# The causal corner of attention: 256 TensorE products replaced by a mask that GpSimd adds into the loaded row of F

## The chip, the cores and the metric

One core of one Trainium2 chip runs the whole program in one launch. The metric is device time in microseconds (us), from the first to the last instruction of the program on that core and what little lies around it. Five engines with a queue each matter here: TensorE (PE in the profile, PEld for its weight loads), VectorE (DVE), ScalarE (ACT), GpSimd (POOL) and the DMA queues, above all that of SyncE (SP). Each engine takes its instructions in the order of its queue. An instruction that needs another engine's result waits on a semaphore, and everything behind it in the same queue waits with it.

## The reference

The program is one layer with two branches, a Mamba-2 branch and an attention branch with 16 heads of 64, over 1024 positions and 1024 channels. Only the attention branch is touched. Cut to what matters:

```
fcum = jnp.cumsum(log_f, axis=-1)
for blk in range(seqlen // ATT_BLOCK):                 # 8 blocks of 128 queries
    q0, q1 = blk * ATT_BLOCK, (blk + 1) * ATT_BLOCK
    s = jnp.einsum('bhqd,bhkd->bhqk', q[:, :, q0:q1], k[:, :, :q1]).astype(jnp.float32) * scale
    s = s + fcum[:, :, q0:q1, None] - fcum[:, :, None, :q1]
    qpos = q0 + jnp.arange(ATT_BLOCK)
    kpos = jnp.arange(q1)
    s = jnp.where(kpos[None, :] <= qpos[:, None], s, -jnp.inf)
    prob = jax.nn.softmax(s, axis=-1)
    outs.append(jnp.einsum('bhqk,bhkd->bhqd', prob.astype(v.dtype), v[:, :, :q1]))
```

A block of 128 queries sees all earlier key blocks whole. Only in its own block, the last 128x128 corner of its scores, must the keys that lie after a query be hidden. That corner is the subject of the change.

## The kernel before

The kernel computes negated scores (q is stored times -0.125), so a hidden key must get a very large positive number, a row's best key is its minimum, and the exponential is taken of minus the score plus that minimum.

Before attention the program computes the projections and the Mamba-2 branch, until about 695 us of the profiled span. Attention then takes the heads two by two: `hp` runs from 0 to 7, and e = 0, 1 is the head of the pair, which sits on partitions 0 to 63 or 64 to 127. Inside a pair there are six groups, given by `GROUPS`: a pair of query blocks (`u` = 0 is the higher block, `u` = 1 the lower) against one half h of the keys, 512 positions. Four of the six groups are diagonal ones, where both query blocks meet their own key block: g0 (blocks 7 and 6, upper keys, 512 and 384 keys wide), g2 (blocks 5 and 4, upper keys, 256 and 128), g4 (blocks 3 and 2, lower keys, 512 and 384) and g5 (blocks 1 and 0, lower keys, 256 and 128). Groups g1 and g3 lie fully below the diagonal. So there are 32 diagonal groups in the program, and 48 in all.

One group goes through these steps. `scores` multiplies on TensorE (in three products, since q and k are each split into two parts) into PSUM tiles `s`, one for each e, first for u = 0 and then for u = 1. VectorE then runs one combined instruction for each (u, e), line 1459: it adds `fb`, the row of F for these keys, which was loaded from memory and repeated over all 128 partitions, writes `ex`, and leaves the row's minimum in `nm`. ScalarE takes the exponential in place and sums it (line 1463). `turned` transposes `ex` on TensorE into tiles `pt`, which VectorE (line 1481) or ScalarE (line 1483) copy to `p`, and `weighted` multiplies them with v into `av`. The transposes of the first key block need the four `ex` of the group in the order u0 e0, u0 e1, u1 e0, u1 e1.

So that TensorE is not idle while VectorE and ScalarE work on a group, the program puts pieces of an independent stream of matrix products between the steps: `fill(m, 0)` between the scores and the transposes, `fill(m, 1)` between the transposes and `weighted`. Such a piece is called a half: six products 512 wide. The stream needs its own copies on the other engines, which share their queues with attention: ScalarE empties PSUM (`s<-pb`, line 404) and rounds weights (`wop<-raw`, `wop<-sum`, line 351), VectorE forms the remainders (line 352) and sums (lines 357, 373, 381) and combines results (lines 414 to 418); in the later head pairs it also splits operands (`x..h`, `x..l`, lines 277 to 281).

A softmax needs the sums over both key halves. `send` transposes the factors (`tp`), ScalarE copies them (`st`), GpSimd sends them to memory (`st_dram`, line 1387), SP loads them back repeated (`rb`, line 1393), and VectorE multiplies the output with them (lines 1418 and 1424, then 1425 for `zr`). Two groups after the scores this must be done. GpSimd also writes `zr` to memory (`ya_dram`, line 1514), forms differences of blocks (lines 213, 1520, 1526, 1527, 1540) and stores them (line 195, 1060).

The causal corner is made on TensorE: after the three products of a diagonal tile come two more products for each e, 64 rows by 128 columns in bf16, of a piece of the unit matrix `eye` with a piece of `far`, which holds 1e30 above the diagonal. They add the corner to the scores in PSUM (lines 1447 to 1453). `eye` and `far` are made once, at lines 1293 to 1306.

A scheduler in the language sets the order of each engine's queue from the program's order and its own estimate of times. Instructions that go through `pin` or `mm` keep the program's order among themselves; the others, those of the stream among them, are placed by the scheduler, so that a change of the program can move them.

## Time and profile before

| what | value |
|---|---|
| median of 3 runs | 1339.51 us (1337.2 to 1344.38) |
| profiled execution, span from first to last instruction | 1338.1 us |
| TensorE busy | 1273.1 us, 95% of the span |
| VectorE busy | 1016.8 us, 76% |
| ScalarE busy | 787.4 us, 59% |
| GpSimd busy | 303.6 us, 23% |
| the 256 corner products (`s<-far,eye`) | 18.6 us busy, mean 225 ns |
| mean granted TensorE clock | 0.988 |

The page gives no time of the profiled execution other than its span, 1.4 us under the median. Busy times of TensorE are sums over pipelined instructions: the next product starts before the one ahead has ended, so what a product costs is read from start to start and not from its length. A row of the timeline has the start, the length, engine, line, operation and tiles, how many like instructions were merged into it, and in brackets the idle time of the engine ahead of it with what ended it. A row of the table by stretches has for each engine the busy time and the count of its instructions.

### The profile page before, as it was taken

Reading aid. Unit: us, or ns where it says so; the run is one execution under the profiler, and the core shown is the slowest. Engines: PE = TensorE matmul, PEld = TensorE weight load, DVE = VectorE, ACT = ScalarE, POOL = GpSimd, SP = SyncE. Lnnn points to the kernel's source line nnn. Section 1 sums busy time; section 2 is a strip of 40 time slices with the busy share of each in tenths; the row PEclk is TensorE's granted clock in tenths of the full one; section 3 lists DMA queues with packets and bytes.
Section 4 is the critical chain, followed back from the end, with each engine's and each line's share of the span. In section 5 each row is a group of like instructions: output and inputs, shape, how many; then the busy total and the mean of one; then the engine's idle time right before and its main releaser. Section 6 shows DMA issues by size and latency. Waiting matters only on the chain. (4 is left out here: it accounts for less than half of the span.)

```text
span 1338.1 us, 21044 instructions
## 1 busy us (share of the span) xinstructions
PE 1273.1 (95%) x7054; PEld 992.6 (74%) x7054; DVE 1016.8 (76%) x1977; ACT 787.4 (59%) x1726; POOL 303.6 (23%) x311
## 2 busy tenths in 40 slices
PE   6899999999999999999999999998879998889997
PEld 4678878777888888788877777776657666668886
DVE  7979986887888888888676667666876657676976
ACT  7645765466665666566556665666754545543664
POOL 3000440013300431034002132221121213235152
PEclk9999999999999999999999999999999999889999
DMA  7232543554446533654474566567855657545933
GB/s 287 70 116 66 164 136 121 155 171 157 127 126 202 166 120 121 198 170 130 135 267 151 180 201 204 183 228 241 277 194 185 189 190 244 182 149 183 368 127 102
DMA packets 154668, 233.59 MB, mean 175 GB/s; under 512 B 17216, under 2 KB 62656, under 8 KB 154560
## 3 DMA queue, kind: packets, MB, share of 16 engines
q1 hardware_dynamic: 142016, 205.53, 48.2%
q0 software_dynamic: 6400, 16.10, 3.2%
q10 hardware_dynamic: 6144, 10.62, 2.1%
q8 instruction: 55, 0.90, 0.3%
q14 instruction: 53, 0.43, 0.1%
HBM read 162.99 MB, written 72.34 MB: 176 GB/s over the span
## 5 line engine op out<-in xcount | busy, mean ns | idle before, releaser
L1463 ACT ACTIVATE ex<-ex,nm 128x512 f32<-128x512 f32 (+1 forms) x192 | 116.0, 605 | 154.2 <-DVE nm L1459 152.3
L352 DVE TENSOR_TENSOR wop<-sum,wop 128x512 fp32r<-128x512 f32 x180 | 138.3, 769 | 54.5 <-ACT wop L351 53.4
L351 ACT ACTIVATE wop<-sum 128x512 fp32r<-128x512 f32 x180 | 112.4, 625 | 78.1 <-DVE sum L357 29.6
L352 DVE TENSOR_TENSOR wop<-raw,wop 128x512 fp32r<-128x512 f32 x144 | 110.5, 768 | 43.6 <-ACT wop L351 42.6
L404 ACT ACTIVATE s<-pb 128x512 f32<-128x512 f32 x144 | 84.9, 589 | 90.2 <-PE pb L130 87.8
L130 PE MATMUL pc<-x3h,wop 128*128 128x512 f32 x384 | 133.1, 404 | 2.8 <-DVE th L414 1.7
L130 PE MATMUL pc<-x2h,wop 128*128 128x512 f32 x384 | 130.9, 399 | 2.3 <-DVE th L416 2.0
L130 PE MATMUL pb<-x4h,wop 128*128 128x512 f32 x384 | 130.3, 396 | 2.8 <-ACT x4h L277 2.1
L130 PE MATMUL pb<-x0h,wop 128*128 128x512 f32 x384 | 132.3, 401 | 0.0
L130 PE MATMUL pb<-x5h,wop 128*128 128x512 f32 x384 | 130.7, 399 | 1.0 <-ACT s L404 1.0
L130 PE MATMUL pb<-x6h,wop 128*128 128x512 f32 x384 | 129.0, 394 | 0.0
L1459 DVE CUSTOM_DVE_ANT_0 ex<-s,fb 128x512 f32<-128x512 f32 (+1 forms) x192 | 95.7, 550 | 36.8 <-PE s L130 36.8
L133 PE MATMUL pt<-ident,ex 128*128 128x128 f32 x576 | 81.3, 283 | 20.5 <-ACT ex L1463 19.8
L351 ACT ACTIVATE wop<-raw 128x512 fp32r<-128x512 f32 x144 | 89.5, 622 | 12.4 <-PE pc L130 6.1
L130 PE MATMUL pd<-x1h,wop 128*128 128x512 f32 x288 | 96.6, 394 | 0.0
L133 PEld LDWEIGHTS pt<-ident,ex 128*128 128x128 f32 x576 | 67.7, 143 | 35.9 <-ACT ex L1463 29.9
L130 PEld LDWEIGHTS pc<-x3h,wop 128*128 128x128 f32 x384 | 73.7, 192 | 22.0 <-issue 2.6
L130 PEld LDWEIGHTS pc<-x2h,wop 128*128 128x128 f32 x384 | 72.1, 188 | 20.8 <-DVE th L416 3.1
L130 PEld LDWEIGHTS pb<-x5h,wop 128*128 128x128 f32 x384 | 73.3, 191 | 18.5 <-ACT s L404 1.7
L130 PEld LDWEIGHTS pb<-x4h,wop 128*128 128x128 f32 x384 | 72.1, 188 | 19.7 <-ACT x4h L277 2.5
L130 PEld LDWEIGHTS pb<-x0h,wop 128*128 128x128 f32 x384 | 73.5, 191 | 16.3 <-issue 0.9
L130 PEld LDWEIGHTS pb<-x6h,wop 128*128 128x128 f32 x384 | 72.1, 188 | 16.1 <-issue 0.4
(310 smaller groups left out, 2965.8 us busy)
## 6 DMA issues: line engine op xcount, KB each, us to landing
raw<-in_wu SPq DMA_DIRECT2D x128, 256.0 KB, 4.1
csb<-cs_dram SPq DMA_DIRECT2D x32, 256.0 KB, 5.2
fb<-f_dram SPq DMA_DIRECT2D x16, 512.0 KB, 6.2
rb<-st_dram SPq DMA_DIRECT2D x48, 128.0 KB, 3.1
wd<-in_wo SPq DMA_DIRECT2D x40, 128.0 KB, 3.1
xt<-in_x SPq DMA_DIRECT2D x8, 512.0 KB, 5.9
gs_dram<-th ACTq DMA_DIRECT2D x16, 256.0 KB, 3.7
qh_dram<-th SPq DMA_DIRECT2D x16, 256.0 KB, 2.0
```

The source lines that it names most:

```text
L130: return tc.keep_in_program_order(nc.tensor.matmul(*args, **kw))
L133: return tc.keep_in_program_order(nc.tensor.transpose(out_, in_, idn))
L351: nc.scalar.activation(op[:, 0], src, AF.Copy)
L352: nc.vector.tensor_tensor(op[:, 1], src, op[:, 0], ALU.subtract)
L404: nc.scalar.activation(s, ps, AF.Copy)
L1459: nc.vector.tensor_tensor_reduce(o, s[e][:, 0:w], fb[hp, h][:, e, 0:w], 1.0, 3.0e38, ALU.add, ALU.min, nm)
L1463: pin(nc.scalar.activation(o, o, AF.Exp, scale=-1.0, bias=nm, accum_out=hd.at(hd.sm, i, h, e)))
```

## The change

The corner is no longer added by TensorE. A tile `ahead` (128x128, float) holds 1e30 above the diagonal and zero elsewhere. The new function `hide` lets GpSimd add it in place into one 128-key block of the row `fb`, for one e or for both. VectorE's combined instruction then adds `fb` as before, and the mask comes with it.

Since the same row of F serves two query blocks, the moment matters: the block that is the corner for u = 0 must already be masked when u = 0 is read, and the block that is the corner for u = 1 must be masked after u = 0 has read it unmasked and before u = 1 reads it. So in each diagonal group there are two half-size additions (one for each e, 128x128) between VectorE's reads for u = 0 and u = 1, 64 in all. And there are 32 full additions (both e, 128x2x128) ahead of the groups: after the scores of g0, of g3 and of g4 for later groups of the same pair, one more after g4 for the next pair's first group, and one before the loop. What is masked stays masked: a later group of the pair does not read such a block, or needs it masked.

```
-        eye = ap.tile([P, 192], BF16, name="eye")
-        far = ap.tile([P, 192], BF16, name="far")
-        nc.vector.memset(eye, 0.0)
-        big, beyond = small("big"), small("beyond")
-        nc.vector.memset(big[:, 0:192], -NEG)
-        for e in range(2):
-            nc.vector.tensor_copy(eye[rows[e], 64:P], ident[rows[e], rows[e]])
-            nc.gpsimd.affine_select(
-                beyond[:, 192 * e : 192 * e + 192], big[:, 0:192], [[1, 192]], ALU.is_gt, 0.0, base=64 * e - 64,
-                channel_multiplier=-1,
-            )
-            nc.vector.tensor_copy(far[rows[e], :], beyond[rows[e], 192 * e : 192 * e + 192])
-        corner = [(eye[:, 64:192], far[:, 64:192]), (eye[:, 0:P], far[:, 0:P])]
+        ahead = ap.tile([P, P], F32, name="ahead")
+        big = small("big")
+        nc.vector.memset(big[:, 0:P], -NEG)
+        nc.gpsimd.affine_select(ahead, big[:, 0:P], [[1, P]], ALU.is_gt, 0.0, base=0, channel_multiplier=-1)
+
+        def hide(hp, h, block, es=slice(0, 2)):
+
+            f = fb[hp, h][:, es, block * P : block * P + P]
+            pin(nc.gpsimd.tensor_tensor(f, f, ahead.unsqueeze(1).to_broadcast([P, es.stop - es.start, P]), ALU.add))
...
-            diagonal = h == i // 4
             for m, (x, y) in enumerate(ops):
                 for e in range(2):
-                    mm(
-                        s[e][:, 0:w], x[rows[e]], y[rows[e]], start=(m == 0), stop=(m == 2 and not diagonal),
-                        skip_group_check=True,
-                    )
-            if diagonal:
-                for n, (x, y) in enumerate(corner):
-                    for e in range(2):
-                        mm(
-                            s[e][:, w - P : w], x[rows[e]], y[rows[e]], start=False, stop=(n == 1),
-                            skip_group_check=True,
-                        )
+                    mm(s[e][:, 0:w], x[rows[e]], y[rows[e]], start=(m == 0), stop=(m == 2), skip_group_check=True)
...
                 pin(nc.scalar.activation(o, o, AF.Exp, scale=-1.0, bias=nm, accum_out=hd.at(hd.sm, i, h, e)))
+                if u == 0 and h == i // 4:
+                    hide(hp, h, pair[1] % 4, slice(e, e + 1))
...
             load_v(0, h)
+        hide(0, 1, 3)
         for _ in range(14):
             stream.half()
...
             stream.release()
+            if g in (0, 4):
+                hide(hp, GROUPS[g][1], 1)
+            if g == 3:
+                hide(hp, 0, 3)
+            if g == 4 and hp + 1 < NK:
+                hide(hp + 1, 1, 3)
             for hd, which in end(m):
                 hd.settle(which)
```

The scheduler's order also changes. In the rows below, `ex,sm<-ex,nm` is the exponential, and `x2` says that two like instructions follow each other. ScalarE's queue at the first diagonal group (pair 0, g0), before:

```order
L1463 ACTIVATE ex,sm<-ex,nm 128x512 x2
L1463 ACTIVATE ex,sm<-ex,nm 128x384 x2
L404 ACTIVATE s<-pb 128x512
L351 ACTIVATE wop<-raw 128x512
L1483 ACTIVATE p<-pt 128x512 x2
```

And with the change, where the exponential is at line 1445 and the copy at line 1467:

```order
L1445 ACTIVATE ex,sm<-ex,nm 128x512 x2
L1445 ACTIVATE ex,sm<-ex,nm 128x384
L404 ACTIVATE s<-pb 128x512
L351 ACTIVATE wop<-raw 128x512
L1445 ACTIVATE ex,sm<-ex,nm 128x384
L1467 ACTIVATE p<-pt 128x512 x2
```

Two instructions of the stream now stand ahead of the group's last exponential. The same pair of instructions is moved so in pair 1, g0; in pair 6, g0 four are moved (`s<-pb`, `wop<-raw`, `th<-pb`, `wop<-raw`), two ahead of the third exponential and two ahead of the fourth; in g4 of pairs 0 to 4 and 6 one.

GpSimd's queue around pair 5, g0, before (`ya_dram<-zr` is the output's way to memory, `x` and `y` are block differences):

```order
L1060 DMA ms_dram<-th 128x512
L1514 DMA ya_dram<-zr 128x512
L1526 TENSOR_TENSOR x<-zr,x 128x512
L1527 TENSOR_TENSOR y<-x,y 128x512
L195 DMA t_a<-x 128x512
L195 DMA t_a<-y 128x512
```

And with the change, where 128x128 rows of line 1301 are the half-size additions and 128x2x128 the full ones:

```order
L1301 TENSOR_TENSOR fb<-fb,ahead 128x128 x2
L1498 DMA ya_dram<-zr 128x512
L1510 TENSOR_TENSOR x<-zr,x 128x512
L1511 TENSOR_TENSOR y<-x,y 128x512
L1301 TENSOR_TENSOR fb<-fb,ahead 128x128 x2
L1301 TENSOR_TENSOR fb<-fb,ahead 128x2x128
L195 DMA t_a<-x 128x512
L195 DMA t_a<-y 128x512
```

The two half-size additions of g0 stand behind `ya_dram`, `x` and `y`, which all wait for `zr`. The same holds in g0 of pairs 6 and 7.

VectorE's queue in pair 5, g0 (`ISA ex,nm` is the combined instruction, `ISA nm` its short second part), before:

```order
L1459 ISA ex,nm<-s,fb 128x512
L1459 ISA nm 128x1
L1459 ISA ex,nm<-s,fb 128x512
L1459 ISA nm 128x1
L357 TENSOR_TENSOR sum<-sum,raw 128x512
L1459 ISA ex,nm<-s,fb 128x384
L1459 ISA nm 128x1
L1459 ISA ex,nm<-s,fb 128x384
L1459 ISA nm 128x1
L381 TENSOR_TENSOR raw<-raw 128x512
```

And with the change, where the combined instruction is at line 1441:

```order
L1441 ISA ex,nm<-s,fb 128x512
L1441 ISA nm 128x1
L357 TENSOR_TENSOR sum<-sum,raw 128x512
L1441 ISA ex,nm<-s,fb 128x512
L1441 ISA nm 128x1
L381 TENSOR_TENSOR raw<-raw 128x512
L1441 ISA ex,nm<-s,fb 128x384
L1441 ISA nm 128x1
L1441 ISA ex,nm<-s,fb 128x384
L1441 ISA nm 128x1
```

The second sum of the stream (`raw<-raw`) has moved from behind the group's combined instructions to ahead of the last two. In pair 4, g2 an operand split moves in the same way.

## The prediction

> **What bounds the kernel now.** I read the table by stretches first, one row for each pair of heads in attention (start to end in us, then busy time of PE, PEld, DVE, ACT and POOL).
>
> ```profile
> 695.50:752.60 57.10, 57.10 (x391) 43.70 (x390) 36.57 (x99) 35.82 (x90) 8.15 (x10) 1.00 0.51 162
> 868.30:927.20 58.90, 57.54 (x393) 43.68 (x391) 39.42 (x101) 37.51 (x95) 13.82 (x18) 1.00 0.66 218
> ...
> 927.20:991.80 64.60, 54.25 (x359) 38.24 (x355) 48.93 (x119) 43.82 (x108) 9.34 (x14) 0.97 0.71 244
> 991.80:1051.60 59.80, 54.46 (x363) 39.13 (x361) 39.69 (x102) 28.98 (x80) 12.68 (x19) 0.97 0.57 189
> ...
> 1111.90:1176.00 64.10, 54.51 (x344) 38.53 (x342) 44.72 (x111) 36.98 (x96) 19.50 (x23) 0.92 0.64 210
> ```
>
> TensorE is busy 57.10 of 57.10 us in pair 0 and still 57.54 of 58.90 in pair 3: there a TensorE instruction less is time saved. In pairs 4, 5 and 7 it stands idle for 10.4, 5.3 and 9.6 us, and something else sets the pace. The table of waits for 927 to 1176 us says what (waiter, awaited: us, times, longest):
>
> ```profile
> PE pt L133 <- ACT ex L1463: 19.8, 28, 2.8
> ```
> ```profile
> DVE o L1424 <- DMA rb<-st_dram: 12.1, 5, 3.1
> ```
>
> TensorE waits for the exponentials, and these are late because VectorE first waited for the softmax factors on their way through memory. There a shorter TensorE step mostly makes a longer wait.
>
> **What goes: the corner products.** The timeline of TensorE in pair 0, at g0, g1 (no corner) and g2:
>
> ```profile
> 695.52 0.97 PE L130 MATMUL s<-k,q 64*128 64x512 f32 x6
> 696.33 0.29 PE L130 MATMUL s<-far,eye 64*128 64x128 bf16 x4
> 696.42 0.77 PE L130 MATMUL s<-k,q 64*128 64x384 f32 x6
> 697.03 0.29 PE L130 MATMUL s<-far,eye 64*128 64x128 bf16 x4
> 697.25 0.50 PE L130 MATMUL pb<-x4h,wop 128*128 128x512 f32 x1
> ...
> 706.15 1.67 PE L130 MATMUL s<-k,q 64*128 64x512 f32 x12
> 707.75 0.50 PE L130 MATMUL pb<-x5h,wop 128*128 128x512 f32 x1
> ...
> 717.06 0.62 PE L130 MATMUL s<-k,q 64*128 64x256 f32 x6
> 717.52 0.29 PE L130 MATMUL s<-far,eye 64*128 64x128 bf16 x4
> 717.62 0.53 PE L130 MATMUL s<-k,q 64*128 64x128 f32 x6
> 717.99 0.29 PE L130 MATMUL s<-far,eye 64*128 64x128 bf16 x4
> 718.21 0.50 PE L130 MATMUL pb<-x0h,wop 128*128 128x512 f32 x1
> ```
>
> From the first score product to the first of the stream, g0 takes 1.73 us, g1 1.60 and g2 1.15. Six products 512 wide take 0.81 (695.52 to 696.33), 384 wide 0.61, 256 wide 0.46, 128 wide 0.37. Without a corner g0 should take g1's time less the difference of one set, 1.60 - 0.20 = 1.40, and g2 1.60 - 0.35 - 0.44 = 0.81. So a corner costs 0.33 or 0.34 us; since part of each set's time is the change-over to the corner, I take 0.30. Four groups in eight pairs: 32 x 0.30 = 9.6 us, between 0 (all turned into waits) and 10.9 (32 x 0.34). The setup lost (two casts, two memsets for one) lies 15 us ahead of the first group, beside other work: nothing.
>
> **What comes: 64 half-size and 32 full additions on GpSimd.** No such shape is in the trace; the nearest are a GpSimd addition or product of 256 elements and one of 512.
>
> ```profile
> 571.84 0.41 DVE L839 TENSOR_TENSOR xdt<-tr,dtn 128x256 f32<-128x256 f32 x1
> ```
> ```profile
> 572.33 0.61 POOL L871 TENSOR_TENSOR xe<-xdt,tend 128x256 f32<-128x256 f32 x1 [13.82 <-DVE xdt L839]
> ...
> 581.62 1.06 POOL L892 TENSOR_TENSOR new<-new,cdec 128x256 f32<-128x256 f32 x1
> ...
> 929.12 1.29 POOL L213 TENSOR_TENSOR x<-x,th 128x512 f32<-128x512 f32 x1
> ```
> ```profile
> L1300 POOL TENSOR_SCALAR_AFFINE_SELECT beyond<-big 128x192 f32<-128x192 f32 x2 | 0.6, 346 | 48.0 <-DVE th L636 48.0
> ```
> ```profile
> 678.63 0.66 DVE L1304 CAST far<-beyond 64x192 bf16<-64x192 f32 x2 [0.45 <-POOL beyond L1300]
> ```
>
> 256 elements take 0.61 us (1.06 at worst here) and 512 take 1.29, so a full addition (256) costs 0.61 and a half-size one, by the same slope, 0.29, since nothing on VectorE that reads two SBUF tiles need stand beside it; at most 0.61. GpSimd started `xe` 0.08 us after VectorE ended `xdt` (572.25). VectorE started `far` 0.03 us after the first `beyond` ended (678.25 + 0.35). A half-size addition is thus back 0.08 + 0.29 + 0.03 = 0.40 us after VectorE has read the row. The time it has for that stands in VectorE's ladder at g0 and g2:
>
> ```profile
> 697.62 0.68 DVE L1459 CUSTOM_DVE_ANT_0 ex<-s,fb 128x512 f32<-128x512 f32 x1
> ...
> 698.23 0.69 DVE L1459 CUSTOM_DVE_ANT_0 ex<-s,fb 128x512 f32<-128x512 f32 x1
> ...
> 698.84 0.55 DVE L1459 CUSTOM_DVE_ANT_0 ex<-s,fb 128x384 f32<-128x384 f32 x1
> ```
> ```profile
> 717.89 0.41 DVE L1459 CUSTOM_DVE_ANT_0 ex<-s,fb 128x256 f32<-128x256 f32 x1
> ...
> 718.23 0.42 DVE L1459 CUSTOM_DVE_ANT_0 ex<-s,fb 128x256 f32<-128x256 f32 x1
> ...
> 718.58 0.29 DVE L1459 CUSTOM_DVE_ANT_0 ex<-s,fb 128x128 f32<-128x128 f32 x1
> ...
> 718.79 0.28 DVE L1459 CUSTOM_DVE_ANT_0 ex<-s,fb 128x128 f32<-128x128 f32 x1
> ```
>
> The e = 0 read of g0 ends at 698.30, its masked row is back at 698.70, and u = 1 starts at 698.84 anyway: no wait. At g2 it ends at 718.30, is back at 718.70, and 718.58 was the start: 0.12 us late; e = 1 is back at 718.65 + 0.40 = 719.05 for 718.79: 0.26 late. So g2 and g5 lose 0.26 us on VectorE. In pairs 0 to 3 TensorE has other work then; in pairs 4, 5 and 7 it waits for these exponentials: 6 x 0.26 = 1.6 us.
>
> **What is moved.** ScalarE's end of the first group, and TensorE's transposes after it:
>
> ```profile
> 700.38 0.60 ACT L1463 ACTIVATE ex<-ex,nm 128x384 f32<-128x384 f32 x1
> ...
> 700.98 0.58 ACT L404 ACTIVATE s<-pb 128x512 f32<-128x512 f32 x1
> 701.45 0.62 ACT L351 ACTIVATE wop<-raw 128x512 fp32r<-128x512 f32 x1
> ```
> ```profile
> 701.47 1.69 PE L133 MATMUL pt<-ident,ex 128*128 128x128 f32 x14
> ```
>
> The fourth transpose needs the last exponential; at 1.69/14 = 0.12 us each that is about 701.8, and it was ready at 700.98, 0.8 us ahead. The change lets VectorE do a sum (0.61 by the ladder's step) ahead of u = 1, and ScalarE `s<-pb` (0.47) and `wop<-raw` (0.6) ahead of the last exponential. VectorE's delay uses some 0.4 that ScalarE had left over, so the exponential is ready about 1.4 to 1.5 us later, near 702.4. TensorE then waits instead of saving: 0.6 us lost and 0.3 not gained. Pair 1, g0 has the same move, and I count the same 0.6. In pair 6, g0 `th<-pb` also stands ahead; it needs a bank that TensorE finishes just ahead of the transposes, and I count 1.4. Together 2.6 lost, 0.9 not gained: 3.5 us. The six moves in g4 (one instruction, 0.5 to 0.6 us) I cost at nothing: one such move stays within the 0.8 us of room found in g0; without that cover they cost 6 x 0.55 = 3.3. The moved sum in pair 5, g0 and the moved split in pair 4, g2 lie where TensorE waits: 2 x 0.6 = 1.2 us.
>
> GpSimd's queue is the other place. In g0 of pairs 5 to 7 the half-size additions stand behind `ya_dram`, `x` and `y`:
>
> ```profile
> 1116.97 1.27 POOL L1527 TENSOR_TENSOR y<-x,y 128x512 f32<-128x512 f32 x1
> ```
> ```profile
> 1116.66 0.56 DVE L1459 CUSTOM_DVE_ANT_0 ex<-s,fb 128x384 f32<-128x384 f32 x1
> ```
>
> In pair 7 `y` ends at 1118.24, the mask is there at 1118.56, and u = 1 would have started at 1116.66: 1.9 us of VectorE standing still, with all its queue. ScalarE already had two stream instructions (1.1 us) ahead of its last exponential there, so I put 0.8 on the path. Pair 6 is in the 1.4 above. What stands behind the additions on GpSimd is mostly the sending of the softmax factors, and this waits for ScalarE with GpSimd idle:
>
> ```profile
> POOL st_dram L1387 <- ACT st L1385: 146.9, 20, 22.9
> ```
>
> So the additions, which are due before these factors exist, cost it nothing. SP's loads move by one to three places, ten or so of them, all for a later group: nothing; no DMA is added.
>
> The full additions start right behind u = 1, when VectorE goes on with stream work:
>
> ```profile
> 928.75 2.22 DVE L352 TENSOR_TENSOR wop<-raw,wop 128x512 fp32r<-128x512 f32 x1
> ```
>
> This instruction, 0.68 elsewhere, stretched by 1.5 us while GpSimd ran the `x` of 929.12 (1.29 us): VectorE lost all of GpSimd's time. If every full addition did that, 32 x 0.61 = 19.5 us of VectorE's time; where TensorE waits (12 of them, pairs 4, 5, 7) 7.3. Not each meets such an instruction; of 7.3 I put a fifth, 1.4, on the path. [...]
>
> **The sum.** -9.6 for the corners; of these 3.6 back in pairs 4, 5 and 7 (12 x 0.30); +3.5 for ScalarE's moves in g0; +1.6 for the late masks of g2 and g5; +1.2 for VectorE's moves; +0.8 for pair 7; +1.4 for the full additions. That is +2.5 on the profiled span of 1338.1, so 1340.6; the median of the runs stands 1.4 above that span, so 1342.
>
> **The rivals.** Faster: the saving passes nearly everywhere, since the exponentials of g0 keep their room and the late pairs follow TensorE after all; 9.6 less 1.6 is 8, giving 1331. For it speak pairs 0 to 3, where TensorE never stands still; against it the g0 orders above. Slower: the mask comes back late. If a half-size addition takes the 0.61 us of the 256-element row, e = 0 is back 0.72 us after its read and e = 1 0.61 later; u = 1 is late by 0.3 in g0 and g4 and by 0.8 to 0.9 in g2 and g5. Over the 12 groups in which TensorE waits that is 6.9 us for 1.6, and a full addition of 1.29 doubles the 1.4: 1342 + 5.3 + 1.4 = 1349. It decides from about 0.43 us for a half-size addition, when 0.54 us between two reads of g0 no longer cover it. For it speaks the row of 1.06 us; against it the shapes beside the combined instruction. That the change does nothing of what it says is excluded by TensorE's queue, which has lost all 256 products.
>
> **How the numbers follow.** A measurement of this kernel can tell about 0.5% (6.7 us) from no change. My sum, near zero from two sides of some 10 us, gets 0.47; the faster rival 0.18; the slower one, with the lock in the late pairs, 0.35, more than the faster because each term of loss was bounded by the room of one profile. The time is 1342. The range goes from the faster rival, 1331, to a little past the slower one, 1351; my own case alone would be 1335 to 1346.
>
> **What would show it.** Right: the corner groups take about 1.4 and 0.8 us from scores to stream; half-size additions of 0.3 us; TensorE as full in pairs 0 to 3 as now except after g0 of pairs 0 and 1, where it waits for the last exponential; longer TensorE waits in pairs 4 to 7; VectorE waiting for `fb` in g0 of pairs 6 and 7. Wrong: half-size additions over 0.43 us; VectorE instructions of 1.3 us and more behind every full addition; or no TensorE wait at g0 at all.

## The result and the profile after

The changed kernel takes 1352.13 us (median of 4 runs, 1346.71 to 1354.81), the kernel before 1338.36 beside it. The ratio is 1.0099, with a 95% interval of 1.0074 to 1.0124: about 1% slower. The prediction was 1342 with a range of 1331 to 1351. The profiled execution of the changed kernel is the shortest of the four, with a span of 1345.0 us against 1338.1 before. So the traces show about 7 of the 13.8 us between the medians.

The table by stretches of the changed kernel, pairs 0, 1, 3, 4, 5 and 7, and then all of attention up to the start of pair 7's last group (start to end in us, its length, then busy time of PE, PEld, DVE, ACT and POOL with counts; the third number from the end is the granted TensorE clock):

```profile
694.89:752.65 57.76, 56.38 (x359) 42.99 (x358) 36.11 (x97) 35.43 (x89) 14.85 (x22) 1.00 0.49 156
752.65:815.97 63.32, 59.23 (x362) 44.42 (x360) 41.63 (x104) 36.33 (x93) 19.96 (x29) 0.97 0.57 183
...
874.19:932.78 58.59, 56.62 (x361) 42.92 (x360) 41.49 (x101) 37.45 (x95) 20.13 (x30) 1.00 0.65 222
932.78:998.06 65.28, 56.05 (x325) 39.62 (x324) 49.91 (x119) 43.69 (x108) 16.69 (x26) 0.90 0.71 240
998.06:1060.26 62.20, 55.53 (x331) 40.40 (x329) 41.73 (x105) 29.30 (x80) 20.30 (x31) 0.92 0.55 182
...
1118.14:1177.52 59.38, 48.29 (x287) 34.22 (x285) 41.91 (x98) 33.55 (x84) 24.26 (x32) 0.94 0.67 222
694.89:1177.52 482.63, 443.18 (x2720) 328.22 (x2719) 330.61 (x825) 284.22 (x724) 156.37 (x231) 0.96 0.61 201
```

The same row for all of attention in the kernel before:

```profile
695.52:1171.04 475.52, 446.02 (x2968) 329.95 (x2967) 321.54 (x825) 283.34 (x724) 104.43 (x138) 0.98 0.62 204
```

Attention is 7.1 us longer, and nothing else differs: before it both need 695 us, after it 164. TensorE is busy 2.8 us less, not 9.6, and stands idle 39.45 us instead of 29.50. The granted clock fell from 0.98 to 0.96. The trace's record of it has stretches of 3.41 us at 0.50, in attention six before and ten after; two that follow each other make one of 6.83. Only the time in which TensorE worked in them can be lost, and half of that is: eleven transposes in a row take 2.61 us in one of them, 0.24 each, where fourteen at full clock took 1.69, 0.12 each. The sums over these stretches alone (their length, then the busy times), in the kernel before and then in the changed one:

```profile
sum 20.47, PE 19.47 PEld 14.13 DVE 12.80 ACT 11.56 POOL 4.16; mean PE 3.89 PEld 2.83 DVE 2.56 ACT 2.31 POOL 0.83
sum 34.14, PE 27.28 PEld 21.80 DVE 19.32 ACT 20.66 POOL 10.54; mean PE 4.55 PEld 3.63 DVE 3.22 ACT 3.44 POOL 1.76
```

So 9.7 and 13.6 us were lost. (Half of the whole stretches, as the expectations below count, is 10.2 and 17.1; that takes in time in which TensorE stood idle anyway.) TensorE's work at full clock is 446.02 - 9.7 = 436.3 before and 443.18 - 13.6 = 429.6 after. The account of attention is then:

| us, from the profiles | before | after | difference |
|---|---|---|---|
| TensorE's work at full clock | 436.3 | 429.6 | -6.7 |
| TensorE idle | 29.5 | 39.4 | +9.9 |
| lost at half clock | 9.7 | 13.6 | +3.9 |
| attention | 475.5 | 482.6 | +7.1 |

Read from start to start and at full clock, the corner products had taken 9.6 us of the work. The transposes `pt` take 2.4 us more than before, and everything else 0.5 more. Where a wait breaks their row up, a transpose that starts alone is 0.33 us long, while the 14 in a row of the kernel before took 1.69 us together, 0.12 each.

TensorE's timeline at the score stages of pair 0, g0 and g2, in the changed kernel:

```profile
694.89 1.50 PE L130 MATMUL s<-k,q 64*128 64x512 f32 x12
696.32 0.50 PE L130 MATMUL pb<-x4h,wop 128*128 128x512 f32 x1
```
```profile
717.96 0.90 PE L130 MATMUL s<-k,q 64*128 64x256 f32 x12
718.79 0.50 PE L130 MATMUL pb<-x0h,wop 128*128 128x512 f32 x1
```

From scores to stream, g0 takes 1.43 us and g2 0.83. The forecast was 1.40 and 0.81. The groups of instructions on GpSimd, by shape (count, busy time, mean ns):

```profile
L1301 POOL TENSOR_TENSOR fb<-fb,ahead 128x128 f32<-128x128 f32 x64 | 31.5, 502 | 95.5 <-DVE nm L1441 93.3 <-DVE ns L1370 1.0 <-DVE sm L1367 0.2
...
L1301 POOL TENSOR_TENSOR fb<-fb,ahead 128x256 f32<-128x256 f32 x32 | 23.2, 734 | 47.9 <-DVE nm L1441 40.5 <-DMA fb<-f_dram 7.4
```

A half-size addition takes 0.50 us where I took 0.29, a full one 0.73 for 0.61. The table of waits for pairs 4 to 7:

```profile
PE pt L133 <- ACT ex L1445: 24.2, 28, 2.8
...
DVE o L1417 <- DMA rb<-st_dram: 8.5, 5, 3.2
DVE ex L1441 <- POOL fb L1301: 3.6, 9, 1.6
```

VectorE's wait for the factors is 3.6 us shorter than before, and its wait for the masked row, which is new, is as long. TensorE waits 4.4 us more for the exponentials there. The groups g0 of pairs 0, 1, 6 and 7 became 1.5, 4.9, 1.1 and 3.9 us longer; g2 of pair 4 lost 2.1 and g4 of pair 5 lost 1.4. The rows of the four, in the kernel before and then in the changed one:

```profile
695.52:706.15 10.63, 10.63 (x76) 8.12 (x76) 7.48 (x16) 7.72 (x17) 2.09 (x2) 1.00 0.51 160
752.63:763.39 10.76, 10.76 (x77) 8.15 (x75) 6.75 (x17) 7.45 (x18) 3.60 (x5) 1.00 0.61 196
1051.61:1062.67 11.06, 10.89 (x77) 8.15 (x75) 6.42 (x17) 6.17 (x16) 6.28 (x9) 1.00 0.86 267
1111.92:1126.04 14.12, 11.80 (x71) 8.06 (x69) 8.66 (x18) 6.47 (x16) 7.64 (x10) 0.88 0.85 276
```
```profile
694.89:707.03 12.14, 10.76 (x67) 8.02 (x66) 7.56 (x16) 7.83 (x17) 3.34 (x4) 1.00 0.47 135
752.65:768.35 15.70, 12.80 (x69) 9.50 (x67) 9.51 (x19) 8.20 (x19) 5.56 (x8) 0.89 0.45 152
1060.26:1072.38 12.12, 10.65 (x69) 8.07 (x67) 6.12 (x15) 6.55 (x16) 7.42 (x11) 1.00 0.74 245
1118.14:1136.16 18.02, 12.34 (x63) 8.94 (x62) 8.00 (x18) 6.53 (x16) 9.19 (x13) 0.81 0.70 236
```

Not every loss lasted. Pair 7 as a whole is only 0.3 us longer, because its g4 took 12.4 us for 16.1, and pair 6 is 2.4 shorter. What is left over from pair to pair is mostly pair 1 with 5.8 us and pair 5 with 2.4.

Pair 1, g0 is 4.9 us longer: TensorE idles 2.9 us there, and has half its clock for 3.4. A part of what held it up is on VectorE and GpSimd. Their timelines there, before and after:

```profile
752.14 0.68 DVE L381 TENSOR_TENSOR raw<-raw 128x512 f32<-128x512 f32 x1
752.75 0.68 DVE L416 TENSOR_TENSOR th<-pc,s 128x512 f32<-128x512 f32 x1
753.35 0.41 DVE L1425 TENSOR_TENSOR zr<-o 128x256 f32<-128x256 f32 x1
```
```profile
753.27 0.42 DVE L1418 TENSOR_TENSOR zr<-o 128x256 f32<-128x256 f32 x1
753.61 0.68 DVE L416 TENSOR_TENSOR th<-pc,s 128x512 f32<-128x512 f32 x1
754.21 2.23 DVE L381 TENSOR_TENSOR raw<-raw 128x512 f32<-128x512 f32 x1
```
```profile
754.58 1.30 POOL L213 TENSOR_TENSOR x<-x,th 128x512 f32<-128x512 f32 x1
```

The new order puts `raw<-raw` behind `zr` instead of ahead of it. `zr` releases GpSimd's `ya_dram` and then `x<-x,th`, and beside that `raw<-raw` takes 2.23 us instead of 0.68. All that follows on VectorE, the scores among it, is that much later. Two stream instructions of ScalarE also stand ahead of the last exponential there; e9 shows below that most of the 4.9 us needs them.

### The profile page after: what moved, and what is told of

The parts are those of the page before. It is cut to its first block, busy times and chain, and to the rows that moved or that the text cites. A ratio compares the mean times of both kernels' runs of the same rounds, so it can differ in the third digit from the quotient of the medians.

```text
span 1345.0 us, 20717 instructions
## 1 busy us (share of the span) xinstructions
PE 1270.1 (94%) x6798; PEld 990.7 (74%) x6798; DVE 1023.2 (76%) x1972; ACT 788.5 (59%) x1726; POOL 361.1 (27%) x406
## 4 chain that ended last, share of the span: by engine, by line
PE 62%; DVE 12%; DMA 11%; ACT 8%; issue 4%; SPq 1%; POOL 1%; DVEq 0%; ACTq 0%; POOLq 0%
PE pb L130 26%; PE pc L130 15%; PE pd L130 5%; PE av L130 4%; PE pt L133 3%; PE s L130 3%; ACT ex L1445 3%; DVE wop L352 2%; PE yps L130 2%; DMA raw<-in_wu 1%; DVE ex L1441 1%; DMA st_dram<-st 1%; DMA qh_dram<-th 1%; PE tr L133 1%; ACT wop L351 1%
## 5 line engine op out<-in xcount | busy, mean ns | idle before, releaser
L1441 DVE CUSTOM_DVE_ANT_0 ex<-s,fb 128x512 f32<-128x512 f32 (+1 forms) x192 | 99.9, 553 | 45.6 <-PE s L130 36.7
L133 PE MATMUL pt<-ident,ex 128*128 128x128 f32 x576 | 88.3, 293 | 29.8 <-ACT ex L1445 28.4
L133 PEld LDWEIGHTS pt<-ident,ex 128*128 128x128 f32 x576 | 70.8, 148 | 48.9 <-ACT ex L1445 43.5
L1301 POOL TENSOR_TENSOR fb<-fb,ahead 128x128 f32<-128x128 f32 (+1 forms) x96 | 54.7, 579 | 143.3 <-DVE nm L1441 133.8
L213 POOL TENSOR_TENSOR wd<-wd 128x256 f32<-128x256 f32 x32 | 36.0, 1125 | 212.3 <-DMA wd<-in_wo 107.9
```

What stands on the lines that cost most here:

```text
L133: return tc.keep_in_program_order(nc.tensor.transpose(out_, in_, idn))
L213: pin(nc.gpsimd.tensor_tensor(t[out_], t[a_], t[b_], ALU.subtract))
L1301: pin(nc.gpsimd.tensor_tensor(f, f, ahead.unsqueeze(1).to_broadcast([P, es.stop - es.start, P]), ALU.add))
L1441: nc.vector.tensor_tensor_reduce(o, s[e][:, 0:w], fb[hp, h][:, e, 0:w], 1.0, 3.0e38, ALU.add, ALU.min, nm)
```

## The experiments

The theories have letters in the expectations. All ratios are to the kernel before, run beside them on the same chip.

| run | median us | ratio | 95% interval |
|---|---|---|---|
| e1, no mask | 1338.27 | 1.0012 | 0.9996 to 1.0029 |
| e2, additions without the wait | 1338.26 | 1.0009 | 0.9991 to 1.0027 |
| e3, corner and additions | 1342.50 | 1.0031 | 1.0011 to 1.0051 |
| e4, select for add | 1356.28 | 1.0139 | 1.0110 to 1.0167 |
| e5, no mask, one corner kept | 1340.98 | 1.0009 | 0.9985 to 1.0034 |
| e6, changed kernel, pinned | 1354.29 | 1.0110 | 1.0089 to 1.0130 |
| e7, e6 and four products | 1350.13 | 1.0088 | 1.0064 to 1.0111 |
| e8, kernel before, pinned | 1346.04 | 1.0062 | 1.0041 to 1.0084 |
| e9, changed kernel, rule | 1337.00 | 0.9995 | 0.9973 to 1.0017 |
| e10, e9 and four products | 1334.68 | 0.9968 | 0.9943 to 0.9993 |
| e11, kernel before, rule | 1332.23 | 0.9958 | 0.9938 to 0.9978 |
| e12, rule, no mask | 1330.38 | 0.9930 | 0.9908 to 0.9953 |
| e13, e10, VectorE adds in g0 | 1333.10 | 0.9974 | 0.9953 to 0.9994 |
| e14, changed kernel, VectorE adds in g0 | 1351.06 | 1.0116 | 1.0085 to 1.0148 |
| e15, e10 without the wait | 1326.42 | 0.9919 | 0.9894 to 0.9943 |
| e16, changed kernel, waits filled | 1342.39 | 1.0041 | 1.0018 to 1.0064 |
| e17, e10, waits filled | 1335.77 | 0.9984 | 0.9964 to 1.0004 |
| e18, e11, waits filled | 1333.93 | 0.9976 | 0.9958 to 0.9994 |

### e1 and e2: what the products are worth, and what the additions cost without a wait

e1 leaves out the line that adds in `hide`. e2 lets the half-size additions write a dead block:

```diff
-            pin(nc.gpsimd.tensor_tensor(f, f, ahead..., ALU.add))
+            d = f if to is None else fb[hp, h][:, es, to * P : to * P + P]
+            pin(nc.gpsimd.tensor_tensor(d, f, ahead..., ALU.add))
...
-                    hide(hp, h, pair[1] % 4, slice(e, e + 1))
+                    hide(hp, h, pair[1] % 4, slice(e, e + 1), pair[0] % 4)
```

> The corner is left out altogether (no products on TensorE, no additions on GpSimd), so the scores above the diagonal are not masked and the output is not the reference's. It gives what the removed products are worth by themselves. My terms: -9.6, of which 3.6 comes back as waits in pairs 4, 5 and 7, so 1338.4 - 6 = 1332. Theory W (the changed kernel is slow because the second query block waits for its masked row, and other work is let in ahead of it) and theory L (the additions on GpSimd lock VectorE wherever they fall) both expect about 1332; a third, M (the shorter score stage itself is worth nothing, what is left over only waits elsewhere), expects 1337 to 1340.

> The changed kernel with every addition at its place and of its size, but the half-size ones read the same block and write a block of the row that nobody reads again; the second query block finds its row unmasked and does not wait. The masks of u = 1 (and of the blocks written) are so left out or misplaced, and the output is not the reference's. Theory W: within 2 us of the kernel without a mask, about 1334. Theory L: the additions still meet VectorE's instructions, so most of the loss stays, 1345 or more.

Both take 1338 us, as long as the kernel before. So the 96 additions themselves cost nothing that can be measured (theory L falls). But the removal of the products gained nothing either, which only theory M had expected. Neither run keeps the order of the changed kernel: with the wait gone, ScalarE's exponentials stand together again in g0 of pairs 0 and 1 in both. So e2 does not tell the wait from the order; e9 and e15 do. The profile of e1 shows where the gain went. TensorE does 6.6 us less work at full clock (429.7) than in the kernel before, but idles 5.5 us more and loses 3.1 more at half clock. A few groups carry it. In pair 1, g0, `raw<-raw` meets GpSimd's `x` with no addition anywhere:

```profile
752.06 2.24 DVE L381 TENSOR_TENSOR raw<-raw 128x512 f32<-128x512 f32 x1
```

In g4 of the same pair the factors are late. SP's waits there, in e1 and then in the kernel before:

```profile
SPq L1385 <- DMA st_dram<-st: 7.0, 1, 7.0
```
```profile
SPq L1393 <- DMA st_dram<-st: 4.8, 1, 4.8
```

### e3 and e4: the wait with the corner in place, and a shorter instruction

e3 keeps the corner products and makes the additions of the changed kernel beside them; ScalarE's order between the exponentials stays as before in all groups but g0 of pairs 6 and 7. e4 replaces the addition of the changed kernel:

```diff
+        def hide(hp, h, block, es=slice(0, 2)):
+
+            f = fb[hp, h][:, es, block * P : block * P + P]
+            pin(nc.gpsimd.tensor_tensor(f, f, ident..., ALU.add))
```

```diff
-            pin(nc.gpsimd.tensor_tensor(f, f, ahead..., ALU.add))
+            n = es.stop - es.start
+            pin(nc.gpsimd.affine_select(f, f, [[0, n], [-1, P]], ALU.is_ge, -NEG, base=0, channel_multiplier=1))
```

> The corner stays on TensorE as before, and GpSimd also adds into the row in place, half-size and full, as in the changed kernel (it adds the identity, which does not hide anything but shifts the score on the diagonal by one, so the output is a little off the reference's). VectorE waits for the row as in the changed kernel, but of the moved ScalarE instructions only those of pair 6 and 7 remain. Theory W: the wait alone costs 0.2 us in g0 and g4 and 0.5 in g2 and g5 on VectorE, which TensorE feels in pairs 4 to 7 only: 1338.4 + about 16 x 0.35 = 1344. Theory L: 1338.4 plus all of the 20 us between the kernel without a mask and the changed one: 1350 to 1358.

> The changed kernel with another instruction for the mask: GpSimd selects (keeps the row up to the diagonal, writes the large number beyond it) instead of adding a second tile. Same places, same waits. By the profile before, a select of 192 elements took 0.35 us, so 128 should take 0.25 where the addition took 0.50; the six moved ScalarE instructions in g4 are not moved with it. Theory W: half of the wait and the moves in g4 go, so about half of the 13.8 us between 1352 and the kernel before comes back: 1343 to 1346. [...]

e3 costs 0.3%, some 4 us, near theory W's 5.6. e4 missed theory W's forecast: a half-size select takes 0.33 us instead of 0.50, and yet it is slower than the addition. In pairs 2 and 3, g4, its selects stand behind stream work on GpSimd that waits for a load. GpSimd's timeline, then VectorE's:

```profile
860.93 1.28 POOL L213 TENSOR_TENSOR th<-x,th 128x512 f32<-128x512 f32 x1 [7.92 <-DMA th<-ys_dram]
```
```profile
863.45 0.56 DVE L1437 CUSTOM_DVE_ANT_0 ex<-s,fb 128x384 f32<-128x384 f32 x1 [2.62 <-POOL fb L1297]
```

These two groups are 3.4 us longer than in the changed kernel, of the 8.6 by which attention is longer in the profile; most of the rest lies in g4 of other pairs and is not traced further. Here the place in GpSimd's queue counted for more than the length of the instruction.

### e5: one corner kept

e5 is e1 with the corner in one group:

```diff
-            diagonal = h == i // 4
+            diagonal = h == i // 4 and (hp, g) == (0, 5)
```

> As the kernel without a mask, but the corner products stay on TensorE in one group, pair 0, g5 (elsewhere the corner is unmasked, so the output is not the reference's). With them VectorE's order ahead of pair 1, g0 is that of before again: raw<-raw stands ahead of zr<-o, and so ahead of GpSimd's x<-x,th, and not behind it. Theory O (what the removal saves is lost again where the new order of instructions meets another engine): pair 1, g0 loses its 3.6 us, and the whole is faster by 3 to 4 us with more products in it, 1334 to 1335. If the lost time of that group has another cause: 1338 or a little more.

The order came back, and with it the group: `raw<-raw` stands ahead of `zr` again.

```profile
750.64 0.68 DVE L381 TENSOR_TENSOR raw<-raw 128x512 f32<-128x512 f32 x1
```

Pair 1 takes 61.3 us for 63.8 in e1. The whole did not get faster (1.0009 for 1.0012), so the forecast of 1334 to 1335 was missed. The place was right, but its 2.5 us are within the intervals, and the late factors in g4 of that pair are still there.

### e6 to e8: the exponentials kept together

ScalarE's `s<-pb` and `wop<-raw` get `pin`, so they can't go ahead of exponentials that the program gives before them. e7 has four products more in pair 0, g5 (overwritten, so that the score stage is as long as before):

```diff
+        attending.append(1)
...
-                nc.scalar.activation(op[:, 0], src, AF.Copy)
+                (pin if attending else (lambda o: o))(nc.scalar.activation(op[:, 0], src, AF.Copy))
...
-                nc.scalar.activation(s, ps, AF.Copy)
+                (pin if attending else (lambda o: o))(nc.scalar.activation(s, ps, AF.Copy))
...
+            if (hp, g) == (0, 5):
+                for x, y in 2 * [(t[:, 0, isl], keys[:, 0, 0:P])]:
+                    for e in range(2):
+                        mm(s[e][:, 0:P], x[rows[e]], y[rows[e]], start=True, stop=True, skip_group_check=True)
```

> The changed kernel with one rule more for the order: ScalarE's stream instructions s<-pb and wop<-raw keep their place behind the exponentials in attention. No stream instruction but one (pair 3, g4) stands between the exponentials of a group on ScalarE then, and VectorE's moves of pairs 0, 4, 5, 6 and 7 are gone as well; the half-size additions and their waits stay. Pair 1, g0 keeps its new order ahead of the scores. Theory O: of the 13.8 us about 8 come back, 1342 to 1345 (no mask, 1338, plus the plain wait of 4 us). Theory W (the late mask itself is what costs): it stays above 1348.

> As the pinned one, and four more products on TensorE in pair 0, g5, whose results are overwritten (they only make that score stage as long as before): VectorE's order ahead of pair 1, g0 is that of before again. Theory O: another 3 to 4 us less, 1338 to 1341, as fast as the kernel before. Theory W: no less than the pinned one without them.

> The kernel before with the same rule for the order, as the thing to compare with: what the rule itself is worth without the change. It takes two instructions from between the exponentials in pair 7, g0 and a few of VectorE's. Both theories: 1336 to 1339; if the rule alone makes it faster, the gain of the pinned kernels is to be read against this one.

All three missed, by the experiment's own fault: the rule ran on past attention. What follows attention in e8, and what TensorE waited for in it:

```profile
1161.86:1341.99 180.13, 158.96 (x691) 126.39 (x689) 121.87 (x182) 83.36 (x170) 64.42 (x47) 0.96 0.50 170
```
```profile
PE pb L130 <- ACT s L406: 12.4, 4, 7.7
```

180 us there for 164. Attention itself took 474.3 us in e6, 467.9 in e7 and 466.0 in e8, for 482.6 in the changed kernel and 475.5 before. This led to the next four.

### e9 to e12: the same rule, in attention only

```diff
             if m == 6 * NK:
+                attending.clear()
                 stream.release()
```

> The pinned changed kernel again, but the rule for ScalarE's order ends with attention. (In the first pinned kernels it ran on into the last projections, where TensorE then waited 12 us for s<-pb and some more elsewhere: the profile of the pinned kernel before shows attention 9.5 us shorter and what follows 16 us longer.) Theory O: the pinned changed kernel's 1354 less 16, 1338, and so 12 to 15 us under the changed kernel, by the order of instructions alone, with the waits for the late mask all in place. Theory W: 1348 or more.

> As e9, with the four overwritten products in pair 0, g5, which give VectorE's old order ahead of pair 1, g0. Theory O: 1350 - 16 = 1334, some 4 us under e9 and faster than the kernel before as it stands. Theory W: as e9 or slower.

> The kernel before with the rule for the length of attention. It is the fair thing to compare e9 and e10 with. Theory O: 1346 - 16 = 1330; with both orders undisturbed the change itself then costs what is left between e10 and this one, the wait for the mask less what the products saved, +2 to +4 us. If the change were a gain in itself, e10 would be under this one.

> The kernel with the rule, and the corner products left out in every group but pair 0, g5 (unmasked corners elsewhere, so the output is not the reference's): VectorE's order ahead of pair 1, g0 is that of before, ScalarE's exponentials stay together. So it is e11 less 31 corners and little else moved, and gives what the products are worth when their removal does not bring a bad order with it. My term was -9.6, of which 3.6 comes back as waits: 6 us under e11, 1324. If the removal is worth nothing even so (the late pairs and the softmax factors' round trip set the pace everywhere that counts): within 2 us of e11.

e9, e10 and e11 came out close to theory O; e12 did not reach its 1324. The changed kernel falls from 1.0099 to 0.9995 by the order alone, with every wait for the mask in place: 1.0%, some 14 us. The rule is worth 0.4% to the kernel before as well. What it is worth more in the changed kernel, 0.62% or about 8 of the 13.8 us, is put down here to the instructions that the change had moved between the exponentials. The four products that restore the order ahead of pair 1, g0 bring another 0.27% (e10), no more than the intervals allow for, and in the traces only 1.2 us of it lie in pair 1. For in e9 `raw<-raw` still meets GpSimd's `x` there:

```profile
749.95 2.23 DVE L383 TENSOR_TENSOR raw<-raw 128x512 f32<-128x512 f32 x1
```

And yet the group takes 12.06 us, for 15.70 in the changed kernel and 10.88 in e10. So 3.6 of the 4.9 us lost there come back with ScalarE's rule, and about 1.2 with the meeting.

With both orders held, the change costs 0.1% (e10, whose interval holds e11's value). e11, the kernel before with the rule, keeps the corner on TensorE and is 0.4% faster than the kernel before and 1.4% faster than the changed one (0.9958 over 1.0099). What the products are worth when no bad order comes with their removal should stand between e11 and e12. It is 6.3 us in the profiled attention (461.6 for 467.9), but 0.28%, some 4 us, by the ratios, whose intervals overlap, and 1.9 us by the medians. My figure was 6, and the other branch, within 2 us, is not excluded. Some dozen of VectorE's instructions also stand in other places in e12.

### e13 to e15: what is left, the wait or the lock

In e10, the half-size additions of pairs 5 and 7, g0, still stand behind `ya_dram`, `x` and `y`, and VectorE waits for them:

```profile
1113.06 0.56 DVE L1448 CUSTOM_DVE_ANT_0 ex<-s,fb 128x384 f32<-128x384 f32 x1 [2.73 <-POOL fb L1303]
```

e13 (from e10) and e14 (from the changed kernel) give those six additions to VectorE. e15 is e10 with the dead block of e2.

```diff
-                    hide(hp, h, pair[1] % 4, slice(e, e + 1))
+                    hide(hp, h, pair[1] % 4, slice(e, e + 1), nc.vector if (hp, g) in ((5, 0), (6, 0), (7, 0)) else nc.gpsimd)
```

> As e10 (the changed kernel with the rule and the four overwritten products), but in g0 of pairs 5, 6 and 7 VectorE makes the half-size additions itself; GpSimd's stand behind ya_dram, x and y there, and VectorE stood still for 2.0 us (pair 5) and 2.7 us (pair 7) for them in e10, with 1.7 us more ladder in pair 6. Nothing else is moved. Theory Q (what is left of the loss is GpSimd's queue): 2.0 + 2.7 less 0.6 us for the two additions in each, and TensorE waits in those groups of pairs 5 and 7, so 3 to 5 us under e10: 1330 to 1332, as fast as the kernel before with the rule (1332) or a little faster. If the wait there is not on the path: 1334 to 1335.

> The changed kernel, without the rule, with the same six half-size additions on VectorE. Theory Q: pair 7, g0 has 5.6 us of ladder in it for 2.25 before, pair 5 3.9, pair 6 4.5; of these about 2, 1 and 2 are GpSimd's queue. TensorE waits in pairs 5 and 7: 3 to 5 us of the changed kernel's 13.8 come back, 1347 to 1349. The rest is in the moved instructions, which stay (theory O). If GpSimd's queue is not the cause: 1352.

> As e10 (rule and four overwritten products), but the half-size additions write a block that nobody reads again, as in e2, so VectorE never waits for them (the masks of u = 1 are left out and those of other blocks are misplaced, and the output is not the reference's). The order of instructions is that of e10 but for one (pair 3, g4), and that of e12. If the wait for the mask (its length of 0.45 us and its place in GpSimd's queue) is what is left: as e12, the kernel without additions, 1330 to 1331, 4 us under e10. If the additions cost by locking VectorE: as e10, 1334 to 1335.

e13 and e14 gained nothing that can be measured (0.9974 for 0.9968, 1.0116 for 1.0099), so theory Q's forecasts were missed. In pair 7 VectorE's own addition met the same two instructions of GpSimd. VectorE's timeline in pair 7, g0 of e13, then GpSimd's:

```profile
1111.12 1.67 DVE L1303 TENSOR_TENSOR fb<-fb,ahead 128x128 f32<-128x128 f32 x1
1112.72 0.68 DVE L1448 CUSTOM_DVE_ANT_0 ex<-s,fb 128x512 f32<-128x512 f32 x1
```
```profile
1111.36 1.28 POOL L1517 TENSOR_TENSOR x<-zr,x 128x512 f32<-128x512 f32 x1
1112.72 1.27 POOL L1518 TENSOR_TENSOR y<-x,y 128x512 f32<-128x512 f32 x1
```

The addition of 128 elements, with two SBUF inputs, took 1.67 us beside `x`. The combined instruction of 512, which reads one input from PSUM, took its usual 0.68 beside `y`. e15 answers the question: without the wait e10 falls from 0.9968 to 0.9919, by 0.5% or 6.5 us where 4 were forecast, and it is as fast as e12, which has no additions at all (0.9930). So the wait for the masked row, its length and its place in GpSimd's queue together, costs some 6.5 us with the order held (the two intervals just meet), and the lock by the additions nothing that can be measured.

### e16 to e18: the waits filled

Four transposes of the identity go ahead of each of the first four transposes, at places where TensorE waits. They are overwritten by the transposes that follow. In e16 ScalarE's order in attention is that of the changed kernel, and of VectorE's instructions nine stand in other places:

```diff
+                        if b == bs[0] and ((hp, g) == (1, 0) or hp in (4, 5, 7) and g in (0, 2, 4) or (hp, g) == (6, 0)):
+                            for _ in range(4):
+                                turn(bank[:, e, t, :], ident)
                         turn(bank[:, e, t, :], ex[:, e, 1 - t, b % 4 * P : b % 4 * P + P])
```

> The changed kernel, and where TensorE waits for the exponentials (g0, g2 and g4 of pairs 4, 5 and 7, g0 of pairs 1 and 6) four transposes of the identity, 0.1 us each, stand ahead of each of the first four transposes; their results are overwritten, and no other instruction moves. Theory C (the waits cost twice, because after them the granted clock is 0.5 for 3.4 us or 6.8 us): in the profile of the changed kernel attention has 34 us at half clock, 17.1 us lost by it, against 10.2 in the kernel before. With the waits filled by work the loss falls to 10 or less although nothing else is faster: 1343 to 1347. If the clock does not follow TensorE's waits: 1352, or more for the 1.6 us of transposes in each of 11 groups where they don't fit into the wait.

> The same transposes in e10 (the changed kernel with the rule and the four overwritten products); its attention loses 11.9 us by the clock. Theory C: 6 or less, so 1328 to 1331, level with the kernel before with the rule (1332) and faster than both kernels. If the clock does not follow the waits: 1335 or more.

> The same in e11 (the kernel before with the rule), in g0, g2 and g4 of pairs 4, 5 and 7. It loses only 5.1 us by the clock in attention, and TensorE waits less. Theory C: at most 3 us to gain, 1329 to 1332; it is the control for the fillers themselves: if they cost time where there is little to wait for, it shows here as more than 1332.

e16 has 176 transposes more on TensorE, some 21 us of useless work at 0.12 us each, and is 9.7 us faster by the medians, 1342.39 for 1352.13, or 8 by the ratios (1.0041 for 1.0099). Its attention, and a wait with its filling in pair 7, g0:

```profile
694.01:1175.97 481.96, 452.01 (x2896) 339.97 (x2895) 331.58 (x825) 285.00 (x724) 156.30 (x231) 0.99 0.62 201
```
```profile
1119.80 0.66 PE L133 MATMUL pt<-ident 128*128 128x128 f32 x4
1120.71 0.33 PE L133 MATMUL pt<-ident,ex 128*128 128x128 f32 x1 [0.25 <-ACT ex L1445]
```

The clock there is 0.99 for 0.96: three stretches of half clock for ten, 4.3 us lost for 13.6. The traces themselves differ by only 0.7 us in attention, since the one of the changed kernel is of its shortest run. But the clock is on record for every run: over the whole program it was 0.988 to 0.995 in the twelve runs of e16 and 0.979 to 0.984 in the four of the changed kernel. So with TensorE's waits filled most of the half clock was gone, though not all of it.

e17 and e18 gained nothing and missed theory C's times. The clock of e17's runs rose too, 0.991 in the mean for 0.987 in e10, and its trace lost 7.5 us by it for 9.4, but its attention is 4.9 us longer. e18 had only the 5.0 us of e11's trace to lose. Where little is waited for, the filling costs as much as it brings.

## Why the prediction was wrong, step by step

**The corners, -9.6.** Right as work: the products had taken 9.6 us of TensorE's time at full clock, and the score stages came out as forecast. Whether 3.6 of it comes back as waits is not settled: with the order held, e12 gained 6.3 us in the profiled attention for my 6, but 2 to 4 in the measured times.

**The sum.** This is the step that failed. Behind the corners it adds terms of waiting and nothing else, together 12.1, and each wait is counted once, at its length. TensorE's idle time grew by 9.9. But a wait cost more than its length: in the profile 3.9 us went to the half clock behind the waits (e16, with waits filled, lost 4.3 by it for 13.6), 2.4 to transposes that start alone instead of in a row (0.33 us for 0.12), and 0.5 to the rest of the work. The rows quoted for the kernel before already had 0.97 and 0.92 in the column of the clock, in pairs where TensorE waits, and 1.00 in the two others. With these 6.8 us the forecast would have been 1342 + 6.8 = 1349.

**Luck in it.** That the idle time comes near the 12.1 is luck. I had put 8.6 of it into pairs 4, 5 and 7, where it grew by 2.8, and 1.8 into pairs 0 and 1, where it grew by 5.3.

**Single terms of it.** The full additions cost nothing that can be measured (e2 against e1, e15 against e12) for 1.4. The late masks were sized on a half-size addition of 0.29 us (the slope of the two rows gives 0.27), and it took 0.50. The point from which I gave the case to the slower rival was 0.43. The late masks and the 0.8 for pair 7 were 2.4 together, and e15 measures 6.5 for the wait, clock included. In pair 7, g0 TensorE idles 3.4 us more, with GpSimd's queue as foreseen, but most of it came back in g4 of the same pair.

**ScalarE's and VectorE's moves, +4.7 together.** Too small: e9 to e11 put 8 us on the rule for ScalarE's order, clock included, and the 3.6 of e10 are within the intervals. Of its places, pair 6, g0 was right in size (TensorE idles 1.3 us more for 1.4). Pair 0, g0 was too small: it is 1.5 us longer for 0.6. Pair 1, g0 was far too small: TensorE idles 2.9 us there, with half clock behind it, and the group is 4.9 us longer for 0.6. The cause that I gave, ScalarE's move, is the larger part by e9; beside it stands VectorE's `raw<-raw`, which moved behind `zr` and met GpSimd's `x`. I had looked for moves between the exponentials and not ahead of them, although the stretched row of 928.75 was in the text as the price of such a meeting. That the g4 moves cost nothing held in pairs 0 and 2, where the group is 0.30 us shorter.

**The rivals.** The faster one fell: even with no additions at all (e1) the removal of the products gains nothing in the order that comes with it. The slower one, 1349, came nearest. Its condition was met, but its mechanism, the late mask, is only a part (6.5 us with the order held); the lock that it adds was not found, and the order is worth more.

**What stays open.** The four executions of the changed kernel lie between 1346.7 and 1354.8, and only the shortest has a trace. What the longer ones lost beside these 7 us is not shown; it is not the clock alone, since one of the two longest had 0.984, the best of the four. By the ratios the 0.99% are 0.62 and 0.27 for the order (e9, e11, e10), 0.49 for the wait (e10 less e15), and -0.39 for the products, the additions being free (e15 less e11). Each of these is uncertain by about 0.2 to 0.3, and they hold for this order of removal: wait and order act on the same exponentials, and e2, which removes the wait and with it most of ScalarE's moves, comes back to the time before by itself.

## What to carry to other kernels

Waits of TensorE cost more than their own length here: up to 1.7 us for each stretch of 3.41 us at half clock behind them (13.6 us were lost at half clock, 9.7 before), and a slower start of the transposes that they separate (0.33 us for 0.12, in all 2.4). Read the clock's column of the stretches beside the waits, before any term of waiting goes into a sum. Where a scheduler sets the order, taking work away moves other work, and the comparison is only fair with the order held; here holding it was worth 0.4% in the kernel before and 1.0% in the changed one, and the change itself then cost 0.1%. A mask that another engine must put in between two reads of the same row can cost its round trip and whatever that engine's queue has ahead of it; here the two together cost some 6.5 us with the order held (e15).

## What was not expected of the hardware

The clock fell to 0.50 behind much less than a full stop. The stretches of pair 1, g0 in the changed kernel, and TensorE's timeline there:

```profile
758.65:762.06 3.41, 0.98 (x3) 0.41 (x3) 2.11 (x8) 3.24 (x9) 2.22 (x4) 1.00 0.26 77
762.06:765.47 3.41, 3.13 (x14) 2.96 (x15) 1.04 (x2) 1.73 (x6) 0.00 (x0) 0.50 0.41 146
```
```profile
759.16 0.33 PE L133 MATMUL pt<-ident,ex 128*128 128x128 f32 x1 [0.70 <-ACT ex L1445]
759.86 0.33 PE L133 MATMUL pt<-ident,ex 128*128 128x128 f32 x1 [0.38 <-ACT ex L1445]
760.74 0.33 PE L133 MATMUL pt<-ident,ex 128*128 128x128 f32 x1 [0.55 <-ACT ex L1445]
762.34 2.61 PE L133 MATMUL pt<-ident,ex 128*128 128x128 f32 x11 [1.27 <-ACT ex L1445]
```

In the 3.41 us ahead of the fall TensorE worked for 0.98, or 29%, in three pieces, and no wait was longer than 1.27 us.

In the traces of the two kernels the half-clock stretches of attention start at whole multiples of 3.41 us from each other. Of the eleven falls in them seven came behind 3.41 us in which TensorE was busy for 19 to 45%, and four behind 3.41 us with 49 to 56%. Among the other stretches at the same spacing, at full clock and with no fall behind them, none was busy for less than 50%, and seven were for 50 to 60%. What decides between the two at 49 to 60% is not shown.

A shorter and simpler mask instruction (e4, 0.33 us for 0.50) made the kernel slower, and useless work on the busiest engine (e16) made it faster. The first goes with a place in a queue, the second with the clock, and neither could be read from the sums of busy time. VectorE was stretched beside one instruction of GpSimd and not beside the next in e13: 1.67 us for an addition with two SBUF inputs beside `x`, and 0.68, unchanged, for the combined instruction with one beside `y`.
